# A hybrid state-space, mLSTM and expert-lookup block on one core: log-sigmoid chain turned to tokens on partitions, table products dealt out in pairs, last norm per tile

## The chip, the cores and the metric

The kernel runs on one core of one Trainium2 chip. The metric is the device time of one execution in microseconds (us), median of three runs. The engines are called as in the profile: PE (TensorE), DVE (VectorE), ACT (ScalarE), POOL (GpSimd) and SP (SyncE, which here only issues transfers).

## What is computed

One decoder layer on 512 tokens, with 16 learned meta tokens ahead of them (T = 528), width 1024, all in float32:

```python
xn = rmsnorm(h, norm1_g)
u_s, x_m, z_m, g_s, g_m = split(xn @ w_in)
y_s = s5_branch(u_s) @ w_ssm_out                       # diagonal complex state space, gelu, GLU
xc  = silu(causal_conv(x_m))                           # 4 taps per channel
q, k, v = blockdiag(xc, wq), blockdiag(xc, wk), blockdiag(x_m, wv)
gates = concat(q, k, v) @ w_if + b_if
log_i, log_f = gates[..., :H], log_sigmoid(gates[..., H:])     # H = 4 heads
h_m = mlstm(q, k, v, log_i, log_f);  h_m = headnorm(sigmoid(z_m) * h_m) + skip * xc
h = h + (sigmoid(g_s) * y_s + sigmoid(g_m) * (h_m @ w_ml_out)) @ w_out
h = h + peer_ffn(rmsnorm(h, norm2_g))                  # 16 of 128*128 experts for each of 8 heads
out = rmsnorm(h, final_norm_g)[:, 16:]
```

The S5 branch makes its transition and input matrices from parameters, in the kernel: tables w1 (inputs to chunk states) and l3 (chunk states to outputs) are outer products of a [128 x 16 x 16] coefficient and powers of the discretized eigenvalue.

## The kernel before, in words

Two functions follow one another. `front` (about 0 to 500 us) holds everything up to the second norm, `peer` the rest. Every float32 product is done as three matmuls on numbers split into a high and a low part (`mm3`, `proj`: high by high, high by low, low by high; lines 82 to 86 and 343 to 346). `wblock` (L156) loads one 128x1024 block of weights into one of two buffers, splits it with ACT (L78, high part) and DVE or POOL (L79, low part); a running number of the block decides between DVE and POOL. Numbers 21 to 28 are the blocks of the GLU (`wglu`), of the S5 output (`wso`) and the first two of z (`wz0`); all of these go to POOL.

Inside `front` the parts that the change touches are, in order of the program:

- `xmproj(b)` (mLSTM input, block b of 8; two PSUM tiles xm, evacuated by DVE with the norm's factor, L430) and `gsgate(b)` (gate of the S5 branch; PSUM tile gs, evacuated by DVE into `mix`, then a sigmoid on ACT, L480). The projections share four PSUM buffers.
- `outer` (L410): six multiplications or sums of [128 x 2048] for w1, later six for l3 (r and i parts, with one scratch tile t), and at L503 a sign change of l3's imaginary part, all on DVE. `l1part` transposes w1 on PE.
- the chunk states: v on PE, `turn` (L507, twice, around two scans) on DVE; then y (tables l1, l2t, l3 by inputs and states) on PE.
- `conv(b)` (L433): three DVE steps (L436), a sigmoid on ACT into one shared scratch tile (profile name qt, L439), one DVE multiplication by it.
- y is copied from PSUM by ACT (`ys`, L567), written to memory (`yd`, L571), read back in another layout (`yt`, L573), and goes through gelu and the GLU (`yg`, `ygh`, `y2h`, `y2l`).
- the gates' weights `wgt` (split in place of a part of the states' tile) and the gate sums on PE (`gate`, L594), from the split conv outputs `xp`.
- after the GLU, the log-sigmoid of four gate rows: a chain of some 20 DVE steps on [4 x 528] tiles (`rwa`, `rwb`, L625 to L639; Abs and Exp on ACT at L626 and L627), two scans (L645, L646), then the S5 output `so` on PE with its DVE evacuations into `mix`, the first z products, and per 128 tokens a short chain `dv`, `crs` on DVE (L688, L689, and a tensor_tensor) whose four results PE transposes into `cbp` (L694 to L697). The mLSTM's v follows on PE (`vm` L740, `v` L748).

In `peer`, three token tiles of 128 go through all 16,384 experts as dense products on PE, key row by key row (`h`, `o`; 128 rows j, each with a 512 KB load of `v` on SP's queue, L1400, a split into vh by ACT and vl by DVE); for the other 128 tokens, POOL gathers rows of u and v (L1015, six buffers), and DVE accumulates them into `ac` (L1029). Loads of the last stage are tied to a row of this loop by `after(ins, j)`, an order without a wait. At the end the o products of the last rows are made tile by tile, and the last norm runs on DVE and ACT for token tiles (0), (1) and (2, 3) together: residual add (L1445), squares with sum (L1446, ACT), product with the gain (L1447), ten one-column steps for the reciprocal root (L91 to L105), scaling of one half on DVE (L1456) and one on ACT (L1454), two output transfers (L1457).

A scheduler orders each engine's instructions from the program's order and from dependences; `later(ins, on)` adds such an order without a wait.

Of the kernel before, what the change touches and what calls it, by code (L numbers as in the profile page):

```python
# [23 lines left out]
P = 128  # L24
# [102 lines left out]
def front(tc, a, dbg, cst, dram, xnp, ident, h2d, gds, x0, qt01, dump, split, mm3, rsqrt, rsqrt_cols):  # L127
# [3 lines left out]
    with es:  # L131
# [24 lines left out]
        def wblock(src, name, nk=NK):  # L156

            raw = wp.tile([P, NK, P], F32, tag="wraw", name=f"{name}_w", bufs=2)
            SY.dma_start(raw[:, :nk] if len(src.shape) == 3 else raw.rearrange("p (b k) n -> p b k n", b=2), src)
            hi = wp.tile([P, NK, P], F32R, tag="whi", name=f"{name}_h")  # L160
            lo = wp.tile([P, NK, P], F32R, tag="wlo", name=f"{name}_l")
            nblk[0] += 1
            i_ = split(hi[:, :nk], lo[:, :nk], raw[:, :nk], GP if nblk[0] == 2 or nblk[0] > 12 and (nblk[0] % 2 or nblk[0] > NG) else V)
# [257 lines left out]
        def xmproj(b):  # L421
            if b % 4 == 0:
                xmt.append(half(f"xmt{b // 4}", f"xmt{b // 4}"))
                xct.append(half(f"xct{b // 4}", f"xct{b // 4}"))
            hi, lo = wblock(a["w_in"][4 + b], f"wx{b}")
            xm, xc = xmt[b // 4][:, b % 4], xct[b // 4][:, b % 4]
            for h in range(2):
                p = pmm(f"xm{b}{h}", (P, T // 2))
                proj(hi, lo, p, lambda k: [x[k // 4][:, k % 4, h * 264:(h + 1) * 264] for x in (xnh, xnl)])
                tt(xm[:, h * 264:(h + 1) * 264], p, nt[:, h * 264:(h + 1) * 264], OP.mult)  # L430
            A.activation(xc, xm, AF.Identity, scale=convw[:, b, 3:4], bias=convb[:, b:b + 1])

        def conv(b):  # L433
            xm, xc = xmt[b // 4][:, b % 4], xct[b // 4][:, b % 4]
            for s_ in (1, 2, 3):
                V.scalar_tensor_tensor(xc[:, s_:], xm[:, :T - s_], convw[:, b, 3 - s_:4 - s_], xc[:, s_:],  # L436
                                       op0=OP.mult, op1=OP.add)
# [35 lines left out]
        def gsgate(b):  # L473
            hi, lo = wblock(a["w_in"][20 + b], f"wgs{b}")
            p = pmm(f"gs{b}")
            for k in range(NK):
                mm3(p, hi[:, k], lo[:, k], xnh[k // 4][:, k % 4, NM:], xnl[k // 4][:, k % 4, NM:], k == 0, k == NK - 1)
            o = mix[b // 4][:, b % 4]
            tt(o, p, nt[:, NM:], OP.mult)
            A.activation(o, o, AF.Sigmoid)  # L480
        for b in range(2):
            xmproj(b)
            l1part(b)
            gsgate(b)

# [6 lines left out]
        for x in range(2):  # L492
            for q0, q1 in ((0, 7), (7, 14), (14, 16)):
# [5 lines left out]
                A.copy(vs[:, x, q0:q1], p[:, :q1 - q0])  # L499
        xmproj(2)  # L500
        gsgate(2)
        outer(*l3, c_r, c_i, pw_r[:, :, 1:], pw_i[:, :, 1:], (OP.subtract, OP.add))
        V.tensor_scalar(l3[1], l3[1], -1.0, None, op0=OP.mult)  # L503

        rt = half("rt", "pBi", (P, 2, NP_, NC_))

        def turn(o, v, sg):  # L507

            for x in range(2):
                tt(o[:, x], v[:, x], phs[0], OP.mult)  # L510
                tt(sct, v[:, 1 - x], phs[1], OP.mult)
                tt(o[:, x], o[:, x], sct, OP.add if (x == 0) == (sg < 0) else OP.subtract)
        turn(rt, vs, -1)
# [3 lines left out]

        st = rt
        turn(st, vs, 1)
        for q in range(4):  # L520
            gkpart(q)
        xmproj(3)
        gsgate(3)
# [97 lines left out]
        dump("ys_glu", yg)  # L621
        rwb = half("rwb", "pE")[:H]
        y2_, z_, lf = (rwb[:, n] for n in range(3))

        later(V.tensor_scalar(xf, xf, bif[:, 1:2], None, op0=OP.add), lo_)  # L625
        A.activation(e_, xf, AF.Abs)  # L626
        A.activation(e_, e_, AF.Exp, scale=-1.0)  # L627
        V.tensor_scalar(y_, e_, 2.0, None, op0=OP.add)
        for h in range(2):
            c = slice(h * 264, (h + 1) * 264)  # L630
            V.reciprocal(y_[:, c], y_[:, c])
        tt(y_, y_, e_, OP.mult)
        tt(y2_, y_, y_, OP.mult)
        V.tensor_scalar(z_, y2_, 1.0 / 15, None, op0=OP.mult)
        for n in (13, 11, 9, 7, 5, 3):
            V.scalar_tensor_tensor(z_, z_, 1.0 / n, y2_, op0=OP.add, op1=OP.mult)
        V.scalar_tensor_tensor(z_, z_, 1.0, y_, op0=OP.add, op1=OP.mult)
        V.tensor_scalar(xf, xf, 0.0, None, op0=OP.min)
        V.scalar_tensor_tensor(lf, z_, -2.0, xf, op0=OP.mult, op1=OP.add)  # L639
        rst, fl, mr = e_, y_, y2_  # L640
        V.memset(rst, 1.0)
        ST = [0] + [NM + i * P for i in range(NT)] + [T]
        for s0 in ST[:-1]:
            V.memset(rst[:, s0:s0 + 1], 0.0)
        V.tensor_tensor_scan(fl, rst, lf, 0.0, op0=OP.mult, op1=OP.add)  # L645
        V.tensor_tensor_scan(mr, lf, li, 0.0, op0=OP.add, op1=OP.max)  # L646
        dump("li", li)
        dump("lf", lf)
        dump("mr", mr)
        tt(li, li, fl, OP.subtract)  # L650
        em = z_
        tt(amu, fl, mr, OP.subtract)
        A.activation(em, mr, AF.Exp, scale=-1.0)
        dv = small("dv", (H, NT + 1))
        V.memset(dv, 0.0)
        for b in range(NK):
# [288 lines left out]
def peer(tc, a, out, dbg, cst, dram, xh, xl, blanks, ident, h2d, gds, x0, qt01, dump, split, mm3, rsqrt_cols):  # L945
# [21 lines left out]
    with es:  # L967
# [419 lines left out]
        for j in range(NKEY):  # L1387
# [51 lines left out]

        for of in ((0,), (1,), (2, 3)):  # L1440
            ss = fin.tile([P, 2, 2], F32, name=f"ss3{of[0]}")
            for n, i in enumerate(of):
                y, x = hr[i], op_[i - 1] if i else ac0
                for c in range(2):
                    order(V.tensor_tensor(y[:, cc[c]], x[:, cc[c]], y[:, cc[c]], op=OP.add))  # L1445
                    A.activation(jq, y[:, cc[c]], AF.Square, scale=1.0 / math.sqrt(D), accum_out=ss[:, c, n:n + 1])  # L1446
                order(V.tensor_tensor(sq[i], y, gf, op=OP.mult))  # L1447
            m = len(of)
            rstd = rsqrt_cols(fin, ss[:, 0, :m], m, f"n3{of[0]}", more=ss[:, 1, :m])
            for c in range(2):  # L1450
                for n, i in enumerate(of):
                    o, x, r_ = hr[i][:, cc[c]], sq[i][:, cc[c]], rstd[:, n:n + 1]
                    if c:
                        A.activation(o, x, AF.Copy, scale=r_)  # L1454
                    else:
                        V.tensor_scalar(o, x, r_, None, op0=OP.mult)  # L1456
                    (SY, A)[c].dma_start(out[i * P:(i + 1) * P, cc[c]], o)  # L1457

# [64 lines left out]
```

## Time and profile before

| | us |
|---|---|
| median of three runs | 1733.84 |
| lowest, highest | 1731.15, 1735.12 |
| the profiled execution, its own time | 1735.74 |
| its span from first to last instruction | 1734.0 |
| PE busy, DVE busy, POOL busy, ACT busy | 1661.3, 1329.4, 722.7, 707.9 |

The time of an execution is that of the device, the span lies 1.7 us below it. The busy times are sums over the whole span; the kernel has stages with different limits, so they are a first look only.

### The profile page before, as it was taken

The page shows a single profiled execution, that of the slowest core. Times are in us where ns is not written, and L with a number is a line of the kernel's source. Part 1 is how long each engine was busy: PE and PEld are TensorE (multiplying, and loading weights), DVE is VectorE, ACT ScalarE, POOL GpSimd, SP SyncE. Part 2 cuts the span into 40 slices and gives each one's busy share as a digit, 9 for nine tenths or more (in the row PEclk, how much of TensorE's full clock was granted, in tenths as well). Part 3 has the DMA queues.
Part 4 walks back from the last instruction along what each step waited for, and adds up shares of the span by engine and source line. Part 5 has one row for each costly group of instructions (what it writes and reads, how often), then busy time and mean ns, then how long its engine had stood idle before and what let it go on. Part 6 is the DMA issues. An engine that isn't in the chain of part 4 may idle for free.

```text
span 1734.0 us, 25541 instructions
## 1 busy us (share of the span) xinstructions
PE 1661.3 (96%) x9376; PEld 1471.6 (85%) x9376; DVE 1329.4 (77%) x2601; ACT 707.9 (41%) x1037; POOL 722.7 (42%) x494
## 2 busy tenths in 40 slices
PE   7899889999999999999999999999999999999992
PEld 6798677877888899999999988888888888888871
DVE  6996783356468899977884688788888888888888
ACT  4454516543332334456664343333333333333321
POOL 2022532214123278888885134333333333343452
PEclk9999989999999999999999999999999999999996
DMA  4513243212442336689999999999999999999894
GB/s 179 117 50 98 75 157 118 77 49 73 167 182 99 124 73 183 163 265 295 300 303 341 348 348 343 346 339 349 335 346 349 336 344 333 349 336 333 296 343 170
DMA packets 172774, 408.79 MB, mean 236 GB/s; under 512 B 44392, under 2 KB 89576, under 8 KB 171496
## 3 DMA queue, kind: packets, MB, share of 16 engines
q1 hardware_dynamic: 108816, 264.40, 43.2%
q0 software_dynamic: 55328, 134.31, 23.2%
q10 hardware_dynamic: 8504, 8.44, 1.6%
q8 instruction: 73, 1.20, 0.3%
q14 instruction: 53, 0.43, 0.1%
HBM read 359.81 MB, written 47.28 MB: 235 GB/s over the span
## 4 chain that ended last, share of the span: by engine, by line
PE 80%; DVE 11%; DMA 4%; ACT 2%; issue 2%; POOL 1%; SPq 0%; POOLq 0%; ACTq 0%; DVEq 0%
PE h L82 10%; PE h L85 10%; PE h L86 10%; PE o L85 10%; PE o L86 10%; PE o L82 10%; PE gp L1304 2%; PE q L85 2%; PE q L86 2%; PE q L82 2%; DMA wo<-in_w_out 1%; PE s L820 1%; PE n L829 1%; DMA v<-in_v 1%; PE gm L343 1%
## 5 line engine op out<-in xcount | busy, mean ns | idle before, releaser
L82 PE MATMUL h<-x2h,uh 128*128 128x384 f32 x1024 | 345.6, 337 | 0.0
L86 PE MATMUL h<-x2h,ul 128*128 128x384 f32 x1024 | 343.3, 335 | 0.0
L85 PE MATMUL h<-x2l,uh 128*128 128x384 f32 x1024 | 343.2, 335 | 0.0
L85 PE MATMUL o<-vl,wh 128*128 128x512 f32 x768 | 301.0, 392 | 0.8 <-DVE vl L79 0.8
L86 PE MATMUL o<-vh,wl 128*128 128x512 f32 x768 | 300.0, 392 | 0.0
L82 PE MATMUL o<-vh,wh 128*128 128x512 f32 x768 | 295.8, 391 | 3.4 <-ACT vh L78 3.4
L1238 POOL DMA_INDIRECT gds<-gw,ix x128 | 238.9, 1867 | 47.1 <-issue 36.6
L1015 POOL DMA_INDIRECT g<-in_v,e x128 | 161.2, 1260 | 229.3 <-PE o L86 78.4
L78 ACT ACTIVATE uh<-u 128x1024 fp32r<-128x1024 f32 x128 | 136.0, 1062 | 250.6 <-PE h L85 198.1
L1015 POOL DMA_INDIRECT g<-in_u,e x103 | 130.4, 1266 | 254.5 <-DVE jk L1022 122.1
L79 DVE TENSOR_TENSOR ul<-u,uh 128x1024 fp32r<-128x1024 f32 x128 | 156.4, 1222 | 73.0 <-ACT uh L78 58.8
L78 ACT ACTIVATE wh<-w 128x384 fp32r<-128x384 f32 x128 | 67.1, 525 | 329.5 <-issue 265.8
L85 PEld LDWEIGHTS h<-x2l,uh 128*128 128x128 f32 x1024 | 192.3, 188 | 2.2
L82 PEld LDWEIGHTS h<-x2h,uh 128*128 128x128 f32 x1024 | 192.3, 188 | 2.3
L86 PEld LDWEIGHTS h<-x2h,ul 128*128 128x128 f32 x1024 | 192.2, 188 | 0.7
L82 PEld LDWEIGHTS o<-vh,wh 128*128 128x128 f32 x768 | 144.8, 189 | 33.0 <-ACT vh L78 3.9
L79 DVE TENSOR_TENSOR vl<-v,vh 128x1024 fp32r<-128x1024 f32 x128 | 156.2, 1221 | 18.8 <-ACT vh L78 17.0
L85 PEld LDWEIGHTS o<-vl,wh 128*128 128x128 f32 x768 | 144.8, 189 | 30.1 <-DVE vl L79 1.1
L86 PEld LDWEIGHTS o<-vh,wl 128*128 128x128 f32 x768 | 144.9, 189 | 29.9
L1029 DVE SCALAR_TENSOR_TENSOR ac<-g,w,ac 128x1024 f32<-128x1024 f32 x127 | 162.6, 1280 | 2.3 <-DMA g<-in_v,e 1.2
L78 ACT ACTIVATE vh<-v 128x1024 fp32r<-128x1024 f32 x128 | 133.5, 1046 | 15.2 <-PE o L86 9.8
L79 DVE TENSOR_TENSOR wl<-w,wh 128x384 fp32r<-128x384 f32 x128 | 71.5, 558 | 84.6 <-ACT wh L78 81.6
(526 smaller groups left out, 3089.8 us busy)
## 6 DMA issues: line engine op xcount, KB each, us to landing
u<-in_ut SPq DMA_DIRECT2D x128, 512.0 KB
v<-in_v SPq DMA_DIRECT2D x128, 512.0 KB
gd<-stg SPq DMA_DIRECT2D x8, 2048.0 KB
gi<-gd SPq DMA_DIRECT2D x16, 1024.0 KB
ad<-act SPq DMA_DIRECT2D x80, 192.0 KB
acl<-ad SPq DMA_DIRECT2D x80, 192.0 KB
gds<-qt SPq DMA_DIRECT2D x8, 1024.0 KB
gi<-gds SPq DMA_DIRECT2D x16, 512.0 KB
```

What stands on the lines that cost most here:

```text
L78: A.activation(hi, src, AF.Copy)
L79: return eng.tensor_tensor(lo, src, f32(hi), op=OP.subtract)
L82: i_ = PE.matmul(ps, lh, rh, start=first, stop=False)
L85: PE.matmul(ps, lh, rl, start=False, stop=False)
L86: return PE.matmul(ps, ll, rh, start=False, stop=last)
L343: i_ = PE.matmul(ps_, hi[:, k], rh, start=k == 0, stop=False)
L820: PE.matmul(p[:, :w], xk[kk][:, c0:c0 + P], qt[:, kk, T - w:], start=kk == 0, stop=kk == 1)
L829: PE.matmul(p, pm[:, OFF[j] + (i - j) * P:OFF[j] + (i - j + 1) * P], vt[:, j], start=j == 0, stop=False)
L1015: return GP.indirect_dma_start(out=t, out_offset=None, in_=a["u"] if s_ < P else a["v"], in_offset=bass.IndirectOffsetOnAxis(ap=e0[:, c:c ...
L1029: i_ = V.scalar_tensor_tensor(ac0, g, w0[:, c:c + 1], ac0, op0=OP.mult, op1=OP.add)
L1238: i_ = GP.indirect_dma_start(out=gds.rearrange("b i j t -> (b i j t)").unsqueeze(1), out_offset=bass.IndirectOffsetOnAxis(ap=ix[:, c:c + 1 ...
L1304: PE.matmul(p[:, t], o1[:, a_, :, b_], ow[:, n, a_, :, b_], start=n == 0, stop=n == 1)
```

## The change

1. Weight blocks 21 to 28 are split by DVE in place of POOL.
2. The twelve `outer` steps are dealt out in pairs, each pair held behind an evacuation of a projection (two behind xmproj(0), gsgate(0), xmproj(1), xmproj(2), gsgate(2), xmproj(3)). The imaginary part of l3 is made with its sign, so the step of L503 goes. Both `l1part` stand behind xmproj(1).
3. The 24 conv steps are held behind the last step of the second turn (`turned`).
4. The log-sigmoid chain stands right behind the gate sums. PE transposes the [4 x 528] row into five groups of [128 x 4] tokens (the last one overlaps the fourth), the chain runs on [128 x 20], five transposes bring it back. Two scans, `li`, `amu` and Exp follow in program order there.
5. The last o products run by halves of 512 columns, the last norm tile by tile with the gain's product by halves, and four reciprocal roots in place of three. The loads of the residual rows `hr` (4 x 512 KB on SP's queue) are tied to rows 122, 122, 123, 123 of the loop in place of 120.

```diff
-            i_ = split(..., GP if nblk[0] == 2 or nblk[0] > 12 and (nblk[0] % 2 or nblk[0] > NG) else V)
+            i_ = split(..., GP if nblk[0] == 2 or nblk[0] > NG + 8 or 12 < nblk[0] <= NG and nblk[0] % 2 else V)
...
-        def outer(o_r, o_i, x_r, x_i, y_r, y_i, sums):
-            for o, a_, b_, c_, d_, op in ((o_r, x_r, y_r, x_i, y_i, sums[0]), (o_i, x_r, y_i, x_i, y_r, sums[1])):
-                tt(o, every(a_), every(b_), OP.mult)
-                tt(t3, every(c_), every(d_), OP.mult)
-                tt(o, o, t3, op)
-        outer(*w1, bb_r, bb_i, pv_r, pv_i, (OP.subtract, OP.add))
+        outers = [(w1[0], ...), (w1[1], ...), (l3[0], c_r, pw1_r, c_i, pw1_i, OP.subtract),
+                  (l3[1], nc_i, pw1_r, c_r, pw1_i, OP.subtract)]
+        def outer(on):
+            for _ in range(2):
+                later(tt(*outers.pop(0)), on)
...
         for b in range(2):
-            xmproj(b)
-            l1part(b)
-            gsgate(b)
+            outer(xmproj(b))
+            if b:
+                l1part(0)
+                l1part(1)
+            outer(gsgate(b)) if not b else gsgate(b)
...
-        V.tensor_scalar(l3[1], l3[1], -1.0, None, op0=OP.mult)
...
-            conv(b)
+            conv(b, turned)
...
+        xtp = ptr("xtp", (P, 5, H))
+        XC = [0, P, 2 * P, 3 * P, T - P]
+        for n, c0 in enumerate(XC):
+            PE.transpose(xtp[:, n], xf[:, c0:c0 + P], ident[:H, :H])
+        V.tensor_copy(xt_, xtp)
+        A.activation(et_, xtp, AF.Abs)
+        A.activation(et_, et_, AF.Exp, scale=-1.0)
...
+        for n in range(5):
+            PE.transpose(lfp[n // 4][:, n % 4 * P:(n % 4 + 1) * P], xt_[:, n], ident)
+        A.copy(lf[:, :S], lfp[0])
+        V.tensor_copy(lf[:, S:], lfp[1][:, P - NM:P])
...
-                    for n in range(NKEY - LAST, NKEY):
-                        products(i, *ops[n], tc.keep_in_program_order if i else None)
+                    for c in range(2):
+                        for n in range(NKEY - LAST, NKEY):
+                            products(i, *ops[n], tc.keep_in_program_order if i or c else None, (c,))
...
-            after(SY.dma_start(hr[i], h2d[i * P:(i + 1) * P]), NKEY - 8)
+            after(SY.dma_start(hr[i], h2d[i * P:(i + 1) * P]), NKEY - 6 + i // 2)
...
-        for of in ((0,), (1,), (2, 3)):
+        for i in range(NT):
```

ACT around the copies of y (`ys`), where the conv's sigmoids (`qt<-xct`) stand, before:

```order
L439 ACTIVATE qt_68<-xct_1212 128x528 x2
L567 COPY ys<-y_1471 128x8x64
L567 COPY ys<-y_1472 128x8x64
L567 COPY ys<-y_1523 128x8x64
L567 COPY ys<-y_1524 128x8x64
L571 DMA yd<-ys 16x32x64 x4
```

and now:

```order
L573 COPY ys<-y_1470 128x8x64
L573 COPY ys<-y_1471 128x8x64
L443 ACTIVATE qt_68<-xct_566 128x528
L78 ACTIVATE xp_1620<-xct_566 128x528
L443 ACTIVATE qt_68<-xct_1211 128x528
L78 ACTIVATE xp_1620<-xct_566 128x528
L443 ACTIVATE qt_68<-xct_1211 128x528 x3
L573 COPY ys<-y_1522 128x8x64
L573 COPY ys<-y_1523 128x8x64
L577 DMA yd<-ys 16x32x64 x4
```

The sigmoids that before are spread among earlier work now stand between and ahead of the ys copies; the last two ys copies, and behind them the transfers to `yd`, follow the eighth sigmoid.

DVE behind the last GLU product, where the log-sigmoid chain (`rwa`, `rwb`) begins, before:

```order
L625 TENSOR_SCALAR rwa<-rwa,bif 4x528
L638 TENSOR_SCALAR rwa<-rwa 4x528
L628 TENSOR_SCALAR rwa<-rwa 4x528
L631 RECIPROCAL rwa<-rwa 4x264 x2
L181 TENSOR_TENSOR mix_570<-so_1989,mix_570 128x8x64
L181 TENSOR_TENSOR mix_570<-so_2003,mix_570 128x8x64
L181 TENSOR_TENSOR mix_570<-so_2023,mix_570 128x8x64
L181 TENSOR_TENSOR rwa<-rwa 4x528
L181 TENSOR_TENSOR mix_570<-so_2037,mix_570 128x8x64
L181 TENSOR_TENSOR rwb<-rwa 4x528
L641 MEMSET rwa 4x528
L634 TENSOR_SCALAR rwb<-rwb 4x528
```

and now:

```order
L617 COPY rwb<-xtp 128x20
L628 TENSOR_SCALAR rwb<-rwb 128x20
L79 TENSOR_TENSOR wso_l<-wso_w,wso_h 128x1024
L181 TENSOR_TENSOR yg<-yg,sglu_1991 128x512
L620 TENSOR_SCALAR rwb<-rwb 128x20
L621 RECIPROCAL rwb<-rwb 128x20
L181 TENSOR_TENSOR rwb<-rwb 128x20
L79 TENSOR_TENSOR y2l<-yg,y2h 128x512
L181 TENSOR_TENSOR rwb<-rwb 128x20
L624 TENSOR_SCALAR rwb<-rwb 128x20
L626 SCALAR_TENSOR_TENSOR rwb<-rwb 128x20 x6
L627 SCALAR_TENSOR_TENSOR rwb<-rwb 128x20
```

The [4 x 528] steps with their two reciprocals, which stood ahead of the evacuations of `so`, are [128 x 20] steps now, and stand among the last steps of the GLU.

SP's queue at the end (`qt<-in_gf` is the load of the last norm's gain, L1400 and L1416 are the loads of v), before:

```order
L1400 DMA v_16110<-in_v 128x1024
L1427 DMA qt_68<-in_gf 128x1024
L1431 DMA hr_16191<-h2d 128x1024
L1431 DMA hr_16192<-h2d 128x1024
L1431 DMA hr_16193<-h2d 128x1024
L1431 DMA hr_16194<-h2d 128x1024
L1400 DMA v_16122<-in_v 128x1024
```

and now:

```order
L1416 DMA v_16123<-in_v 128x1024
L1444 DMA qt_68<-in_gf 128x1024
L1416 DMA v_16135<-in_v 128x1024
L1448 DMA hr_16204<-h2d 128x1024
L1448 DMA hr_16205<-h2d 128x1024
L1448 DMA hr_16206<-h2d 128x1024
L1448 DMA hr_16207<-h2d 128x1024
```

The load of v for the last key row has passed the four loads of the residual rows.

## Rows read from the trace of the kernel before

**Rows 1.** The page's busy times: engine, busy us, share, instructions.

```profile
PE 1661.3 (96%) x9376; PEld 1471.6 (85%) x9376; DVE 1329.4 (77%) x2601; ACT 707.9 (41%) x1037; POOL 722.7 (42%) x494
```

**Rows 2.** Busy time by stretch: stretch, its us, PE, PEld, DVE, ACT, POOL, PEclk, DMA share, GB/s.

```profile
72.50:77.60 5.10, 0.40 (x2) 0.02 (x1) 5.10 (x4) 1.01 (x2) 0.00 (x0) 0.99 0.00 0
77.60:84.30 6.70, 6.42 (x15) 4.94 (x16) 6.70 (x8) 1.60 (x3) 0.00 (x0) 0.50 0.47 157
...
214.20:217.40 3.20, 3.18 (x7) 1.99 (x8) 3.20 (x4) 0.00 (x0) 1.17 (x1) 0.50 0.64 237
...
241.30:251.60 10.30, 6.77 (x57) 5.96 (x61) 6.77 (x20) 2.85 (x5) 3.67 (x4) 0.50 0.84 282
```

**Rows 3.** PE's waits, 60 to 90 us, then 200 to 252 us: total us, times, longest.

```profile
PE xm L343 <- DVE mix L181: 4.7, 1, 4.7
...
PE cbp L694 <- DVE crs L181: 5.3, 3, 3.3
PE so L343 <- DVE mix L181: 2.7, 1, 2.7
PE so L343 <- ACT y2h L78: 0.9, 1, 0.9
```

**Rows 4.** DVE's timeline, tables and conv: start, us, instruction, idle before and releaser.

```profile
74.58 2.29 DVE L181 TENSOR_TENSOR w1i<-s5p 128x2048 f32<-128x2048 f32 x1
...
98.37 4.13 DVE L181 TENSOR_TENSOR t<-parb,pw_r 128x2048 f32<-128x2048 f32 x1
...
109.49 1.21 DVE L503 TENSOR_SCALAR l3i<-l3i 128x2048 f32<-128x2048 f32 x1
...
153.70 0.71 DVE L181 TENSOR_TENSOR xct<-xct,qt 128x528 f32<-128x528 f32 x1 [0.77 <-ACT qt L439]
```

**Rows 5.** ACT's timeline from the last conv sigmoid to the gate's weights.

```profile
153.02 0.64 ACT L439 ACTIVATE qt<-xct 128x528 f32<-128x528 f32 x1 [2.13 <-DVE xct L436]
...
155.37 1.07 ACT L567 COPY ys<-y 128x512 f32<-128x512 f32 x2 [0.75 <-PE y L564]
156.48 4.34 ACTq L571 DMA_DIRECT2D yd<-ys  x4
...
164.17 0.23 ACT L78 ACTIVATE wgt<-wgs 128x32 fp32r<-128x32 f32 x1 [7.72 <-DMA yd<-ys]
```

**Rows 6.** PE's timeline, the first gate sums.

```profile
165.50 2.16 PE L594 MATMUL gate<-xp,wgt 128*100 128x264 f32 x16 [0.21 <-DVE wgt L79]
```

**Rows 7.** DVE's timeline at the end of the GLU and the chain's reciprocals.

```profile
202.06 2.42 DVE L181 TENSOR_TENSOR yg<-yg,sglu 128x512 f32<-128x512 f32 x1 [0.83 <-ACT sglu L618]
...
209.50 3.45 DVE L631 RECIPROCAL rwa<-rwa 4x264 f32<-4x264 f32 x2
```

**Rows 8.** The chain that ended last: start, us, piece; v on PE, then the last load of v.

```profile
247.50 3.71 PE v L748 x16
251.97 1.98 PE v L748 x16
...
1669.54 17.47 DMA v<-in_v
```

**Rows 9.** SP's timeline at the end.

```profile
1666.14 2.16 SPq L1431 DMA_DIRECT2D hr<-h2d  x4
1669.54 0.33 SPq L1400 DMA_DIRECT2D v<-in_v  x1
```

**Rows 10.** DVE's timeline at the end: last split of v, accumulations, norm.

```profile
1688.20 1.23 DVE L79 TENSOR_TENSOR vl<-v,vh 128x1024 fp32r<-128x1024 f32 x1 [3.98 <-ACT vh L78]
...
1701.18 10.67 DVE L1029 SCALAR_TENSOR_TENSOR ac<-g,w,ac 128x1024 f32<-128x1024 f32 x8 [1.23 <-DMA g<-in_v,e]
...
1716.68 1.28 DVE L1445 TENSOR_TENSOR hr<-o,hr 128x512 f32<-128x512 f32 x2
...
1721.46 1.28 DVE L1445 TENSOR_TENSOR hr<-o,hr 128x512 f32<-128x512 f32 x2
...
1728.35 0.88 DVE L1456 TENSOR_SCALAR hr<-sq,n32o 128x512 f32<-128x512 f32 x2
```

More of the change, by code (lines that the diff above doesn't have):

```diff
@@ L162, in wblock @@
             nblk[0] += 1
-            i_ = split(hi[:, :nk], lo[:, :nk], raw[:, :nk], GP if nblk[0] == 2 or nblk[0] > 12 and (nblk[0] % 2 or nblk[0] > NG) else V)
+            i_ = split(hi[:, :nk], lo[:, :nk], raw[:, :nk], GP if nblk[0] == 2 or nblk[0] > NG + 8 or 12 < nblk[0] <= NG and nblk[0] % 2 else V)
             if nblk[0] > NG + 6 and blank:
@@ L429, in xmproj, with conv @@
                 proj(hi, lo, p, lambda k: [x[k // 4][:, k % 4, h * 264:(h + 1) * 264] for x in (xnh, xnl)])
-                tt(xm[:, h * 264:(h + 1) * 264], p, nt[:, h * 264:(h + 1) * 264], OP.mult)
+                i_ = tt(xm[:, h * 264:(h + 1) * 264], p, nt[:, h * 264:(h + 1) * 264], OP.mult)
             A.activation(xc, xm, AF.Identity, scale=convw[:, b, 3:4], bias=convb[:, b:b + 1])
-        def conv(b):
+            return i_
+        def conv(b, on):
             xm, xc = xmt[b // 4][:, b % 4], xct[b // 4][:, b % 4]
             for s_ in (1, 2, 3):
-                V.scalar_tensor_tensor(xc[:, s_:], xm[:, :T - s_], convw[:, b, 3 - s_:4 - s_], xc[:, s_:],
-                                       op0=OP.mult, op1=OP.add)
+                later(V.scalar_tensor_tensor(xc[:, s_:], xm[:, :T - s_], convw[:, b, 3 - s_:4 - s_], xc[:, s_:],
+                                             op0=OP.mult, op1=OP.add), on)
             sg = zero[:, :T]
@@ L499, in front @@
                 A.copy(vs[:, x, q0:q1], p[:, :q1 - q0])
[L500 to L503 removed]
+        outer(xmproj(2))
+        outer(gsgate(2))
         rt = half("rt", "pBi", (P, 2, NP_, NC_))
@@ L511, in turn @@
                 tt(sct, v[:, 1 - x], phs[1], OP.mult)
-                tt(o[:, x], o[:, x], sct, OP.add if (x == 0) == (sg < 0) else OP.subtract)
+                i_ = tt(o[:, x], o[:, x], sct, OP.add if (x == 0) == (sg < 0) else OP.subtract)
+            return i_
         turn(rt, vs, -1)
@@ L518, in front @@
         st = rt
-        turn(st, vs, 1)
+        turned = turn(st, vs, 1)
         for q in range(4):
             gkpart(q)
-        xmproj(3)
+        outer(xmproj(3))
         gsgate(3)
@@ L542, in front @@
         for b in range(4):
-            conv(b)
+            conv(b, turned)
         for b in range(4, NK):
             xmproj(b)
-            conv(b)
+            conv(b, turned)
         GP.memset(zero, 0.0)
@@ L597, in front @@
             A.activation(li[:, c], gp[h][64:64 + H], AF.Identity, bias=bif[:, 0:1])
-            V.tensor_copy(xf[:, c], gp[h][96:96 + H])
+            V.tensor_scalar(xf[:, c], gp[h][96:96 + H], bif[:, 1:2], None, op0=OP.add)
             tt(li[:, c], li[:, c], gp[h][0:H], OP.add)
             tt(xf[:, c], xf[:, c], gp[h][32:32 + H], OP.add)
+        rwb = half("rwb", "pE")
+        y2_, z_, lf = (rwb[:H, n] for n in range(3))
+        xt_, et_, yt_, y2t, zt_ = (
+            rwb[:, 3, 5 * H * n:5 * H * (n + 1)].rearrange("p (n h) -> p n h", h=H) for n in range(5))
+        xtp = ptr("xtp", (P, 5, H))
[5 more added lines that the diff above has]
+        A.activation(et_, et_, AF.Exp, scale=-1.0)
+        V.tensor_scalar(yt_, et_, 2.0, None, op0=OP.add)
+        V.reciprocal(yt_, yt_)
+        tt(yt_, yt_, et_, OP.mult)
+        tt(y2t, yt_, yt_, OP.mult)
+        V.tensor_scalar(zt_, y2t, 1.0 / 15, None, op0=OP.mult)
+        for n in (13, 11, 9, 7, 5, 3):
+            V.scalar_tensor_tensor(zt_, zt_, 1.0 / n, y2t, op0=OP.add, op1=OP.mult)
+        V.scalar_tensor_tensor(zt_, zt_, 1.0, yt_, op0=OP.add, op1=OP.mult)
+        V.tensor_scalar(xt_, xt_, 0.0, None, op0=OP.min)
+        V.scalar_tensor_tensor(xt_, zt_, -2.0, xt_, op0=OP.mult, op1=OP.add)
+        lfp = [ptr(f"lfp{n}", (H, S)) for n in range(2)]
+        for n in range(5):
+            PE.transpose(lfp[n // 4][:, n % 4 * P:(n % 4 + 1) * P], xt_[:, n], ident)
+        A.copy(lf[:, :S], lfp[0])
+        V.tensor_copy(lf[:, S:], lfp[1][:, P - NM:P])
+        rst, fl, mr = e_, y_, y2_
+        V.memset(rst, 1.0)
+        ST = [0] + [NM + i * P for i in range(NT)] + [T]
+        for s0 in ST[:-1]:
+            V.memset(rst[:, s0:s0 + 1], 0.0)
+        V.tensor_tensor_scan(fl, rst, lf, 0.0, op0=OP.mult, op1=OP.add)
+        V.tensor_tensor_scan(mr, lf, li, 0.0, op0=OP.add, op1=OP.max)
+        dump("li", li)
+        dump("lf", lf)
+        dump("mr", mr)
+        tt(li, li, fl, OP.subtract)
+        em = z_
+        tt(amu, fl, mr, OP.subtract)
+        A.activation(em, mr, AF.Exp, scale=-1.0)
+        dv = small("dv", (H, NT + 1))
+        V.memset(dv, 0.0)
         mix.append(half("mix1", "mix1", (P, 4, S)))
@@ L621, in front @@
         dump("ys_glu", yg)
[L622 to L655, printed above, removed]
         for b in range(NK):
@@ L1377, in peer, with products @@
         ops = []
-        def products(i, j, wh, wl, vh, vl, pin=None):
+        def products(i, j, wh, wl, vh, vl, pin=None, halves=(0, 1)):
             s_ = slice(i * P, (i + 1) * P)
-            for c in range(2):
+            for c in halves:
                 cc = slice(c * 512, (c + 1) * 512)
@@ L1438, in order @@
             return i_
-        for of in ((0,), (1,), (2, 3)):
[L1441 to L1449, printed above, removed]
-            for c in range(2):
[L1451 to L1457, printed above, removed]
+        for i in range(NT):
+            ss = fin.tile([P, 2], F32, name=f"ss3{i}")
+            y, x = hr[i], op_[i - 1] if i else ac0
+            for c in range(2):
+                order(V.tensor_tensor(y[:, cc[c]], x[:, cc[c]], y[:, cc[c]], op=OP.add))
+                A.activation(jq, y[:, cc[c]], AF.Square, scale=1.0 / math.sqrt(D), accum_out=ss[:, c:c + 1])
+                order(V.tensor_tensor(sq[i][:, cc[c]], y[:, cc[c]], gf[:, cc[c]], op=OP.mult))
+            rstd = rsqrt_cols(fin, ss[:, 0:1], 1, f"n3{i}", more=ss[:, 1:2])
+            for c in range(2):
+                o, x = y[:, cc[c]], sq[i][:, cc[c]]
+                if c:
+                    A.activation(o, x, AF.Copy, scale=rstd)
+                else:
+                    V.tensor_scalar(o, x, rstd, None, op0=OP.mult)
+                (SY, A)[c].dma_start(out[i * P:(i + 1) * P, cc[c]], o)
 def prepare(inputs):
```

8 lines of the change are left out of this document (7 added, 1 removed).

## The prediction, made before the change was run

> **What bounds the kernel now.** I read the page first, then busy time by stretch, then PE's waits, then the timelines of the engines that PE waits for, and the chain of waits for the end. The page [rows 1] has PE busy for 1661.3 us of 1734.0, so only some 70 us can be had anywhere, and they must be looked for where PE stands still or runs slowly. The waits before 260 us are few [rows 3]: 4.7 us for the evacuation of a gate tile into `mix`, 5.3 for `crs`, 2.7 for `mix` again, 0.9 for `y2h`. [...] Later, to the last key row, the change touches nothing; what is gained or lost before it shifts that stage as a whole. At the end, PE is done early and DVE sets the time [rows 10].
>
> **The table products and the conv.** Before, `mix` is evacuated at 76.8 us behind table products of about 2.2 us each [rows 4]; the wait that follows costs PE 4.7 us, and the half clock 6.7 x 0.5 = 3.35 more. In the new order four table products stand ahead of it in place of five, and no conv step; with 2.2 us less for the one and about 0.7 for each conv step, most of the wait goes, and PE reaches y up to 8 us earlier. That gain I cost at **nothing**, because something else is late next. Before, the last ys copies waited 0.75 us for y on PE [rows 5], but the last conv sigmoid was only just ahead of them (153.02). Now that sigmoid is a condition: the last two ys copies stand behind the eighth sigmoid on ACT, and behind them wait the transfers to `yd`, the reading back, the gate's weights and PE's gate sums (165.50, [rows 6]). The round trip from the first of these transfers to the weights is 164.17 - 156.48 = 7.7 us [rows 5], unchanged. So the gate follows the end of the conv, which is the end of DVE's work in this stretch: 153.70 + 0.71 = 154.4 [rows 4].
>
> What moves that end: the sign step goes (-1.2 [rows 4]), and the last idle 0.77 goes. The eight sigmoids share one scratch tile with their multiplications; four of the pairs now stand with nothing between, so 0.64 + 0.71 in series where before only the 0.71 counted: 4 x 0.64 = +2.6. Two DVE steps now stand right behind ACT work that comes late (the low part of a weight block, the turn's first steps behind the copies of the states); each I take at an ACT copy, 1.07 [rows 5], +2.1. The clears of the scans' tile move ahead of the conv; I take half of one 0.71 step [rows 4], +0.4. The conv then ends 3.1 us later. The last sigmoid stands one 0.71 before that end and the two copies (1.07) follow it: 154.4 + 3.1 - 0.7 + 1.1 = 157.9, against 156.4 before. **Term: +1.5.** Bounds: -2.3, if the two late waits do not appear (-2.1) and the POOL collision that makes one table product 4.13 in place of 2.29 goes (-1.8, [rows 4]); +6, if the other four pairs are in series too (+2.6) and the turn loses as much again in waits that the conv steps filled.
>
> **PE's new gap.** Before, PE had 10 us of gate products between y's end and the gate (165.5 - 155.4). Those start 8 us earlier now, while the gate starts later: a gap of about 10 us in front of the gate. [...] **Term: +3.4**, bounds 0 (another engine ends last in the stretch behind it, so that a slow PE costs nothing) and +5.2. [...]
>
> **The log-sigmoid chain.** Before, it runs in front of and among the `so` evacuations, with two reciprocals of 3.45 us [rows 7], and is done too late for `crs`. On [128 x 20] a step has 20 columns in place of 528 and lies in DVE's idle time of the GLU. Of the waits [rows 3] 5.3 + 2.7 = 8.0 go; the 0.9 for `y2h` I leave, since Abs, a table load and Exp now stand ahead of the last `y2h` on ACT. The half clock behind the `mix` wait goes (3.2 x 0.5 = 1.6). The first v products come back to the time of the second, 3.71 - 1.98 = 1.7 [rows 8]. The `yg` product that collides with a POOL split takes 2.42 [rows 7] and would take about the 0.71 of a free step: 1.7. **Term: -13.0.** The eight splits that move from POOL lie beside the GLU, where DVE waits for ACT and PE; if the four that stand among `so` and z each cost a free split, taken as half a 2.29 step [rows 4], 4 x 1.15 = 4.6 are lost (bound -8.4). If the 0.9 goes as well, it is -13.9.
>
> **The end.** The four loads of residual rows stand ahead of v's last load on SP's queue (1666.14 against 1669.54, [rows 9]); that load takes 17.47 us to land [rows 8], and DVE idles 3.98 before it splits it [rows 10]. With v first, the split and all 16 accumulations behind it can start up to 3.98 earlier. A wait of 1.23 for a gather stays, as the six gather buffers still come free one by one. **Term: -4.0**, bounds 0 (the gathers' transfers take the room) and -5.2. The residual rows land late but have until about 1708.
>
> The norm takes 1721.46 - 1716.68 = 4.8 us for one tile alone, and 1728.35 + 0.88 - 1721.46 = 7.8 for the last two together [rows 10]; those become 9.6, +1.8. Halving the gain's product lets DVE reach the root before ACT has summed the second square: an ACT pass over 528 columns takes 0.64 [rows 5], half a pair of DVE steps as much [rows 10], so the wait is a part of 0.64; I take 0.25 for each of four tiles, +1.0. The last scaling on DVE is one half in place of two, -0.4. **Term: +2.4**, bounds +1.2 (no wait) and +3.4 (0.5 for each).
>
> **Sum:** +1.5 + 3.4 - 13.0 - 4.0 + 2.4 = -9.7. From the profiled execution's 1735.74 that is 1726.0; the median of the three runs is 1.9 lower, so the forecast is **1724.1**.
>
> **The rivals.**
> *The new gap gives it all back.* If conv and turn end 10 us later than I think, or PE's slow stretch reaches far into the GLU, the gate's delay eats the chain's gain: 1733.8 - 9.7 + 9.7, about 1731 to 1736. For it: DVE has no idle time before 154 us but the 0.77, so anything that it waits for there is paid. Against: the table pairs now fill that stretch.
> *Slower: the turn without cover.* The 24 conv steps filled DVE's waits in the turn's chain of copies, scans and products; now all stand behind its last step. Each us that DVE then idles ahead of that step arrives at the gate one for one. The point from which this decides is 9.7 us for no gain and 13.2 for a loss beyond what a measurement tells; with 17 us of idle time, all 24 steps at 0.71 uncovered, the time is 1724.1 + 17 = 1741. Against: the order keeps evacuations, table copies and splits in between.
> *The gate is not held.* If the sigmoids keep up and ys goes out as soon as y is there, the 8 us gained at y arrive, and +1.5 + 3.4 fall away: 1724.1 - 12.9 = 1711. Against it stands ACT's order.
> *The residual rows' move does nothing.* Then 4.0 are missing: 1728.1.
>
> **Chances.** A measurement of this kernel tells 0.2%, 3.5 us, from no change. The forecast has 0.62, the idle move at the end 0.14 and the free gate 0.06, all faster by more than that: 0.82. Giving it back has 0.11, the uncovered turn 0.07. The terms' ends all together would be 1713 and 1740; they don't fall together. The range 1715 to 1731.5 takes in the idle move at the end and about half of each unknown; out of it fall most of the free gate, the uncovered turn and half of the give-back, some 0.18.
>
> **What would show it.** Right: no wait of xm for `mix` near 75 us; PE idle for some 10 us ahead of the first gate sum, and PEclk 0.50 behind it; that sum at 166 to 169 us; no waits for `crs`; both first v groups at 2.0 us; the last split of v about 4 us earlier against the end of PE's main loop; four tiles of some 5 us each in the norm. Wrong: a gate before 162 or after 173, `crs` waits that stay, or a last load of v that still lands 17 us after its issue.

## The result, and the profile after

The changed kernel takes 1723.59 us (median of 4 runs, 1721.68 to 1724.69) against 1733.82 for the kernel before: ratio 0.9942, 95% interval 0.9925 to 0.9959, so 10 us faster by the medians. The profiled execution takes 1724.69 us, with a span of 1722.7; it is 11.05 faster than the profiled execution before (1735.74).

The page of the changed kernel, its busy times [rows 1]:

```profile
PE 1656.1 (96%) x9386; PEld 1469.4 (85%) x9386; DVE 1318.6 (77%) x2622; ACT 707.4 (41%) x1038; POOL 708.1 (41%) x486
```

PE's waits from 90 us on, of the changed kernel (total us, times, longest), which answer to [rows 3]:

```profile
PE gate L600 <- DVE wgt L79: 7.4, 1, 7.4
PE xm L346 <- POOL wx_l L79: 2.3, 1, 2.3
...
PE so L343 <- DVE mix L181: 0.4, 1, 0.4
```

The waits for `crs` and `y2h` are gone, that for `mix` at `so` is down from 2.7 to 0.4, and that for `mix` near 75 us is gone too (the longest wait of PE from 60 to 90 us is now 0.2). Two are new: 2.3 us for a POOL split of a weight block, and 7.4 us ahead of the first gate sum. Busy time by stretch (its columns are those of [rows 2]) shows the granted clock behind the first of the two new waits, and in and behind the second:

```profile
122.40:125.60 3.20, 3.20 (x15) 3.20 (x15) 3.20 (x9) 0.83 (x1) 0.00 (x0) 0.50 0.51 164
159.60:167.20 7.60, 0.16 (x2) 0.04 (x1) 0.54 (x4) 0.70 (x4) 0.87 (x2) 0.75 0.90 175
167.20:170.50 3.30, 3.30 (x16) 3.30 (x17) 1.24 (x3) 2.67 (x4) 1.52 (x1) 0.55 1.11 215
170.50:180.00 9.50, 9.50 (x51) 7.96 (x50) 5.71 (x7) 8.11 (x10) 3.95 (x3) 1.00 0.21 62
```

ACT's timeline from the conv's sigmoids to the gate's weights [rows 5], and PE's first gate sum [rows 6]:

```profile
153.47 0.64 ACT L443 ACTIVATE qt<-xct 128x528 f32<-128x528 f32 x1 [0.24 <-DVE xct L181]
155.23 0.65 ACT L443 ACTIVATE qt<-xct 128x528 f32<-128x528 f32 x1 [1.12 <-DVE xct L181]
156.65 0.65 ACT L443 ACTIVATE qt<-xct 128x528 f32<-128x528 f32 x1 [0.78 <-DVE xct L181]
157.20 1.06 ACT L573 COPY ys<-y 128x512 f32<-128x512 f32 x2
158.29 4.37 ACTq L577 DMA_DIRECT2D yd<-ys  x4
...
165.97 0.23 ACT L78 ACTIVATE wgt<-wgs 128x32 fp32r<-128x32 f32 x1 [7.71 <-DMA yd<-ys]
```

```profile
149.88 0.39 PE L570 MATMUL y<-rt,l3i 64*128 64x64 f32 x4
...
167.19 3.51 PE L600 MATMUL gate<-xp,wgt 128*100 128x264 f32 x16 [7.44 <-DVE wgt L79]
```

y is done on PE at 150.3 (155.3 before), yet its last copies start at 157.2, right behind the eighth sigmoid, and each of the last sigmoids waits for a multiplication by the one before it. DVE's timeline, the log-sigmoid chain in its new form and place [rows 7], and the last `crs`:

```profile
204.99 0.28 DVE L621 RECIPROCAL rwb<-rwb 128x20 f32<-128x20 f32 x1
...
206.42 1.25 DVE L626 SCALAR_TENSOR_TENSOR rwb<-rwb 128x20 f32<-128x20 f32 x6
...
231.07 0.67 DVE L181 TENSOR_TENSOR crs<-rwa,dv 4x512 f32<-4x512 f32 x1
```

`crs` is done at 231.7, ahead of PE's first use at 237.3. The chain of work that ended last, at the two v groups [rows 8]:

```profile
239.74 2.15 PE v L764 x16
...
242.46 1.98 PE v L764 x16
```

The end, on SP's queue [rows 9] and on DVE [rows 10]:

```profile
1660.49 0.33 SPq L1416 DMA_DIRECT2D v<-in_v  x1
1664.88 4.97 SPq L1448 DMA_DIRECT2D hr<-h2d  x4
```

```profile
1674.38 1.23 DVE L79 TENSOR_TENSOR vl<-v,vh 128x1024 fp32r<-128x1024 f32 x1 [0.39 <-ACT vh L78]
1675.52 10.60 DVE L1045 SCALAR_TENSOR_TENSOR ac<-g,w,ac 128x1024 f32<-128x1024 f32 x8
1687.03 7.89 DVE L1045 SCALAR_TENSOR_TENSOR ac<-g,w,ac 128x1024 f32<-128x1024 f32 x6 [0.91 <-DMA g<-in_v,e]
...
1697.95 0.69 DVE L1461 TENSOR_TENSOR hr<-ac,hr 128x512 f32<-128x512 f32 x1
...
1703.16 0.68 DVE L1461 TENSOR_TENSOR hr<-o,hr 128x512 f32<-128x512 f32 x1
...
1718.33 0.48 DVE L1470 TENSOR_SCALAR hr<-sq,n33o 128x512 f32<-128x512 f32 x1
```

DVE waits 0.39 in place of 3.98 for the last split of v. A tile of the norm takes 1703.16 - 1697.95 = 5.2 us in place of 4.8.

To tell front and end apart I use one fixed point: the split of v's row 100, from which PE's loop runs at the same pace in every execution (rows 120 and 124 follow it 116.6 and 137.1 us later in all profiles).

| us | before | after | difference |
|---|---|---|---|
| start to split of v's row 100 | 1535.22 | 1526.18 | -9.04 |
| from there (row 100) to the last split of v | 152.98 | 148.20 | -4.78 |
| from the last split to the first residual add | 23.68 | 23.57 | -0.11 |
| from the first residual add to the end of the span | 22.12 | 24.75 | +2.63 |

The front varies between executions of one code by some 5 us in this measure (1521.3 to 1526.2 in four profiles with the changed front), so single terms of it are read from medians or from stretches in which both profiles do the same.

### The profile page after: what moved, and what is told of

It reads as the page before. It is cut to its first block, busy times and chain, and to the rows that moved or that the text cites. A ratio compares the mean times of both kernels' runs of the same rounds, so it can differ in the third digit from the quotient of the medians.

```text
span 1722.7 us, 25574 instructions
## 1 busy us (share of the span) xinstructions
PE 1656.1 (96%) x9386; PEld 1469.4 (85%) x9386; DVE 1318.6 (77%) x2622; ACT 707.4 (41%) x1038; POOL 708.1 (41%) x486
## 4 chain that ended last, share of the span: by engine, by line
PE 85%; DVE 7%; DMA 3%; ACT 2%; issue 1%; POOL 1%; ACTq 0%; POOLq 0%; DVEq 0%
PE h L82 10%; PE h L85 10%; PE h L86 10%; PE o L85 10%; PE o L86 10%; PE o L82 10%; PE gp L1320 2%; PE q L86 2%; PE q L85 2%; PE q L82 2%; DMA wo<-in_w_out 1%; DVE xct L440 1%; PE s L836 1%; PE n L845 1%; PE gm L343 1%
```

## The experiments

All were timed in five rounds beside the kernel before, whose medians were 1733.8 to 1734.2.

**The last norm as before** (`t_norm`):

```diff
-        for i in range(NT):
+        for of in ((0,), (1,), (2, 3)):
...
-                order(V.tensor_tensor(sq[i][:, cc[c]], y[:, cc[c]], gf[:, cc[c]], op=OP.mult))
+                order(V.tensor_tensor(sq[i], y, gf, op=OP.mult))
```

> The changed kernel, with only the last norm put back to the form before: tiles (0), (1) and (2, 3) together. My theory: the norm per tile is the one part of the change that costs. The span from the first residual add to the end was 22.1 us before (1711.88 to 1734.0) and is 24.75 now (1697.95 to 1722.7); four tiles of 5.2 us in place of 4.8, 4.8 and 7.8. Put back, the time falls by 2.6 us, to about 1721.0, and nothing ahead of the norm moves. Rival: smaller last pieces let the output transfers end sooner, so that four chains cost no more than three; then the time stays within 0.7 us of 1723.6.

Measured: 1720.93 (ratio 0.9920, 0.9907 to 0.9933), 2.7 below the changed kernel; from the first add to the end 22.15 us again. That is what was expected: the norm per tile costs what its rows say.

**The residual rows' loads as before** (`t_hr`):

```diff
-            after(SY.dma_start(hr[i], h2d[i * P:(i + 1) * P]), NKEY - 6 + i // 2)
+            after(SY.dma_start(hr[i], h2d[i * P:(i + 1) * P]), NKEY - 8)
```

> The changed kernel, with only the four loads of the residual rows put back to row 120, ahead of the last load of v. My theory: v's last load lands some 4 to 5 us later, DVE idles before its last split as before (about 4 us), all 16 accumulations start that much later: +4.8 us, about 1728.4. Rival: the accumulations are bound by the gathers (POOL's issues and their transfers), of which the residual rows only change the order; then the waits for gathers shrink by what the split loses, and the time rises by under 1.5 us.

Measured: 1724.14 (0.9952, 0.9938 to 0.9967; 1722.31 to 1730.35), only 0.5 above. ACT's timeline of this run, the last split of v:

```profile
1672.10 1.06 ACT L78 ACTIVATE vh<-v 128x1024 fp32r<-128x1024 f32 x1 [3.57 <-DMA v<-in_v]
```

The wait for v's load is back as expected, and the last split comes 151.88 us after row 100's in place of 148.20. The load lands 16.4 us after its issue here; in `t_norm`, which leaves it ahead of the residual rows, ACT's split begins 12.8 us after the issue and has waited for no load. The first residual add comes 2.6 later, not 3.7, as the waits for gathers shrank from 1.3 to 0.2 us. The median shows less than that: my number was missed, and the rival's (under 1.5) was met. Its interval and that of the changed kernel overlap by more than the difference, so this run alone leaves the size open (`log_hr` below gives it).

**The log-sigmoid chain as before** (`t_log`), its lines moved back behind the GLU and to [4 x 528], the rest as changed:

> The changed kernel, with the log-sigmoid chain put back: on [4 x 528], behind the GLU. [...] Rival: part of what the chain gained is owed to the splits moved from POOL to DVE, which no longer collide with crs and yg; then it rises by 6 to 9 us only.

Measured: 1731.32 (0.9985, 0.9976 to 0.9993), 7.7 above the changed kernel: less than I expected (11 to 13 more, 1735 to 1737), and inside the rival's range (6 to 9). PE's waits of this run:

```profile
PE cbp L700 <- DVE crs L181: 5.1, 4, 4.0
...
PE so L343 <- DVE mix L181: 1.9, 3, 1.2
```

They come back, the longest at `mix` is 1.2 in place of 2.7. The chain is three quarters of the whole gain, even beside all other parts.

Why not more? By the rival, the splits that moved from POOL to DVE own a share, and the timeline fits it. DVE in this run:

```profile
201.61 0.68 DVE L181 TENSOR_TENSOR yg<-yg,sglu 128x512 f32<-128x512 f32 x1
...
207.33 3.45 DVE L637 RECIPROCAL rwa<-rwa 4x264 f32<-4x264 f32 x2
```

The last `yg` product takes 0.68 us in place of 2.42 [rows 7], and the reciprocals start 21.1 us behind the first GLU product (186.24) in place of 24.1 (209.50, behind 185.44). Busy time from the first GLU product to the first q product behind the v groups (columns of [rows 2]): before, then `t_log`, `log_only` (described below) and the changed kernel.

```profile
185.44:258.45 73.01, 64.02 (x403) 53.43 (x402) 59.04 (x90) 21.77 (x30) 30.05 (x19) 0.91 0.39 130
186.24:255.58 69.34, 61.96 (x403) 52.07 (x402) 58.38 (x97) 22.06 (x29) 12.74 (x11) 0.95 0.41 137
185.33:247.76 62.43, 62.03 (x413) 52.41 (x412) 44.37 (x84) 21.28 (x31) 29.55 (x19) 0.97 0.45 153
187.77:248.95 61.18, 60.43 (x414) 50.98 (x413) 44.35 (x91) 21.37 (x30) 11.11 (x11) 1.00 0.46 155
```

With the old chain the stretch is 3.7 us shorter when the splits are on DVE; with the new chain 1.2 (3.1 in `w_pool`), where executions of one front differ by 1.6 (61.1 to 62.7). So the two edits seem to take away in part the same waits. No run moves the splits alone.

**The last sigmoids behind the copies of y** (`ys_held`; in the program the conv steps of blocks 4 to 7 move with them; the lines are shortened, their comments are mine):

```diff
-            conv(b, turned)                      # b = 4 to 7, behind xmproj(b)
...
+        for b in range(4, NK):                   # behind the transfers of yd
+            sgd = conv(b, turned, i_)            # its sigmoid: later(..., i_)
...
+            if t_ % 2:
+                later(i_, sgd)                   # yt's transfers on ACT's queue
```

> The changed kernel, with one order turned round: the last four conv sigmoids on ACT stand behind the copies of y and the issues of their transfers, not ahead of them. My theory: the gate's start at 167.2 us is set by the eighth sigmoid on ACT, to which y (done on PE at 150.3) waits, and not by the data that the gate sums read; the first gate sum comes at 157 to 160, PE's gap of 7.4 us in front of it goes with its half clock, and the GLU starts 5 to 9 us sooner: 1715 to 1719. Rival: the gate sums and the GLU need the conv's last blocks anyway, so the wait only moves to the later gate sums (or to the gelu's input, whose reading back now waits for the last sigmoid): less than 2 us gained.

Measured: 1720.64 (0.9920, 0.9907 to 0.9933), 2.9 faster than the changed kernel: more than the rival's 2, less than my 1715 to 1719. Counted from the first y product on PE (134.0 here, 135.4 in the changed kernel's profile), the first gate sum comes 7.7 us earlier (158.1), the GLU 4.7 (181.6), and the first z product 0.4 (223.9). PE's waits of this run:

```profile
PE gate L606 <- DVE xp L79: 2.4, 4, 1.7
PE xm L346 <- POOL wx_l L79: 2.3, 1, 2.3
PE gate L606 <- DVE wgt L79: 2.1, 1, 2.1
```

So ACT's order did hold the gate, as the theory says. But the gain at the end is not what the gate moved. It lies nearer to what PE's waits shrank, from 7.4 to 2.1 + 2.4: the gate sums only moved ahead of products of `gs` that come later now.

**Conv not held behind the turn** (`c_free`; `later` left out of `conv`):

> The changed kernel, with the conv steps no longer held behind the second turn. My theory: DVE's work up to the conv's end is the same sum, so the gate moves little: the four sigmoid and multiplication pairs in series (some 2.6 us) go, the turn and with it y come later, and PE's gap before the gate shrinks. The gate starts 0 to 2.5 us sooner, the time is 1721 to 1724. Rival: the hold is what brings y forward; without it y is late again and DVE and PE both wait, and the time rises by 3 us or more.

Measured: 1723.65 (0.9947, 0.9934 to 0.9960), no change, within what was expected. But the gate does not start sooner: y ends on PE at 159.0 in place of 150.3, and the first gate sum comes at 169.1. The GLU starts at 179.1, 8.7 us sooner than in the changed kernel's profile, the first z product only 1.2. The gap before the gate is gone, and others take its place (2.0 us for `mix`, 1.8 for `xtp`, 1.3 for `y2l`, 1.0 for `rt`).

**Table products as before** (`o_old`; the old `outer`, called twice, and the sign step):

> The changed kernel, with the table products put back (w1's six at once, l3's six and the sign step behind the gate of block 2, none held). [...] Rival: dealing the products out is part of the gain, as PE's lost 8 us reach the gate: 1728 or more.

Measured: 1725.01 (0.9953, 0.9940 to 0.9965), 1.4 above, within what I expected (1723.6 to 1725.5, with up to 4.7 us of waiting near 75 us). That wait is only 1.2 here (the conv steps, which stood ahead of it before, are not back), so this run tests the wait only in part; `log_only`, which has all of it, is the better test.

**Weight splits given back to POOL** (`w_pool`; the old condition in `wblock`):

> The changed kernel, with the splits of the weight blocks 21 to 28 given back to POOL. My theory: of the gain of the log chain's stretch only the collisions depend on them (a yg product of 2.4 us against 0.7, crs steps of 2.4 to 2.8 against 0.2): the time rises by 1 to 3 us. Rival: on DVE the splits take the room of the so evacuations (so's four late evacuations were 1.25 each), so that giving them back frees DVE and gains 1 us or more.

Measured: 1723.44 (0.9936, 0.9923 to 0.9949), no difference: neither the 1 to 3 us that I expected nor the rival's gain. The collisions do come back (a `yg` product of 2.23 us, a scan of 3.38 in place of 1.22), but only waits of 0.7 and 0.6 reach PE.

**Last sigmoids and norm together** (`ys_norm`):

> Both edits together: the last conv sigmoids behind the copies of y, and the last norm in the form before. They touch stages 1500 us apart, so by my theory their gains add: 2.6 us below the first edit alone, 1712.5 to 1716.5 if that one brings what I expect. Rival: the gather stage takes back what the front gives, because the gathers and loads near the end are paced by transfers; then less than the sum.

Measured: 1719.73 (0.9927, 0.9915 to 0.9939). Both stages show their gain in the profile (z at 222.4, 22.17 us from the first add to the end); the median is 0.9 below the first edit alone, outside the expected range, less than 2.6 and within the spread of the two (1719.96 to 1721.73, 1718.36 to 1724.06).

**The log-sigmoid chain alone, on the kernel before** (`log_only`): lines 604 to 650 of the changed kernel put into it in place of the old ones, nothing else.

> The kernel before, with the log-sigmoid chain alone moved behind the gate sums and turned to tokens on partitions; splits, table products, conv and the end as before. My theory by now: PE is the bound of this stretch too, and the time follows the sum of PE's idle and half-clock time; the chain alone removes the waits for mix and crs and the slow spells behind them, 9 to 12 us, and the wait near 75 us stays but is no longer made up by a gap before the gate. So 1722 to 1726, as fast as the whole change but for the end. Rival: table products, conv hold and splits carry a share; then only 5 to 8 us, 1726 to 1729.

Measured: 1722.60 (0.9933, 0.9920 to 0.9946), 11.2 faster than before, as expected. One edit gives as much as the whole change. PE's waits of this run, 50 to 262 us:

```profile
PE xm L343 <- DVE mix L181: 4.7, 1, 4.7
PE xm L346 <- DVE wx_l L79: 1.0, 1, 1.0
PE gate L594 <- POOL xp L79: 0.9, 2, 0.5
...
PE gate L594 <- DVE wgt L79: 0.3, 1, 0.3
```

The 4.7 us for `mix` are there as before, and PE goes through to the gate (0.3 us). In the change, the table products' new places take the 4.7 away, and 7.4 in front of the gate take their place. The edit changes two things at once, the chain's place and its shape, and no run separates them. Summed over the DVE timelines, the chain's steps ahead of the scans are 12.1 us in the old shape (`t_log`) and 3.0 in the new (the changed kernel), so the old shape in the new place would need some 9 us more of DVE, as an estimate; what that costs is open.

**The chain and the residual rows' loads, on the kernel before** (`log_hr`; `log_only` and the one line of `t_hr` turned round):

> The same with the four loads of the residual rows moved behind the last load of v, and nothing else: the two edits that by my theory carry the gain, without the norm per tile, which costs. If they add, it is 2 to 4 us faster than the chain alone, 1719 to 1723, and faster than the whole change by the norm's 2.6. Rival: the residual rows' move is worth under 1 us, as the medians of the undoing had it.

Measured: 1719.35 (0.9905, 0.9891 to 0.9919), 3.3 below the chain alone and 4.2 below the whole change, as expected: the lowest median of all, with two of the change's parts (`ys_norm` is 0.4 behind it, which is no difference).

**The front alone** (`front_only`: loads, last products and norm as before):

> The changed kernel, with the whole end put back (loads, products by tile, norm for (0), (1), (2, 3)). By the two traces the front gives 9.0 us (start of the split of v's row 100: 1535.2 before, 1526.2 now) and the end 2.3 on balance. So 1724 to 1726. Rival: the end is worth nothing (+2.6 of the norm takes all that the loads give): 1723 to 1724.

Measured: 1724.05 (0.9942, 0.9929 to 0.9955), 9.7 faster than before. It lies on the border of both expectations and does not tell them apart.

**The end alone, on the kernel before** (`tail_only`):

> The kernel before, with the changed end alone. By the traces -4.9 for the accumulations' start and +2.6 for the norm: 1731 to 1732.5. Rival: the loads' move gains under 2 us at the end, since the gathers' waits take the rest; then 1733.5 to 1735, no gain or a loss.

Measured: 1732.50 (0.9991, 0.9982 to 1.0000), 1.3 faster, as expected: what the loads give, less the norm (-1.3 - 2.7 = -4.0 for the loads). The profile has 148.20 us from row 100 to the last split, and 24.73 from the first add to the end.

Over all profiles, the last split comes 151.2 to 153.0 us after row 100's where the residual rows are loaded ahead of v (4 profiles), and 148.20 where they are loaded behind it (10 profiles). The first add comes 174.3 to 176.7 against 171.0 to 172.6 us after row 100's split.

## Why the prediction was right

The forecast was 1724.1, the result 1723.6. The mechanisms were right in the main; that the sum is out by only 0.5 is in part luck, since the new gap was priced too high and so was the chain's gain, and the two errors have opposite signs. In the one profile the terms measure +1.7 (table products and conv), +0.6 (gap), -11.8 (chain and splits), -4.9 (loads) and +2.6 (norm); with +0.5 more between the first q product and row 100 that makes -11.3 of span, against -9.7 forecast and 10.2 by the medians.

- **Table products and conv, +1.5.** Right in its mechanism: the last three multiplications wait 0.7 us each for a sigmoid on the same scratch tile, and the gate follows the conv's end. That end came at 158.0 (forecast 157.5), but at 155.7 to 155.8 in three other profiles with the same front (`t_norm`, `t_hr`, `front_only`), so the half microsecond is luck. The two late waits, 2.1 in the sum, were not where the prediction put them: the turn's first step waited 0.18, and 1.70 was lost ahead of the first table product, for ACT's `s5p`. The first gate sum came at 167.2, +1.7, in this profile, and at 164.9 to 165.1 in the three others, 0.5 earlier than before; the term is +1.7 at most.
- **The gain at y at nothing.** Right as far as the medians tell: `front_only` with the dealt products is no faster than `log_only` without them (1724.05 and 1722.60). The reason was put too narrowly, though. A shift of the gate is not passed on in full: with the gate 7.7 us earlier (`ys_held`) the end came 2.9 earlier. What fits the runs better is PE's time without work or at half clock: 4.7 + 3.35 us went near 75 us, and 7.4 + 2.3, in this profile each with a short stretch at half clock, came.
- **PE's new gap, +3.4.** Over-priced. The 3.4 is half of the 6.7 us at a clock of 0.50 behind the wait near 75 us, and the bound of 5.2 half of the 10.3 around the `crs` waits [rows 2]; no run shows that a gap ahead of the gate costs either. What the profile shows is a stretch at half clock behind the gap of 3.3 us in place of 6.7 (2.8 to 6.2 in the three others), and from the first gate sum to the GLU it took 20.58 us against 19.94, +0.6 (20.3 to 21.6 in the three others, +0.3 to +1.7). The rows show where the rest went: over the 7.6 us around the wait the granted clock is 0.75, over the first 3.3 us of work 0.55, and 1.00 behind them, so a part of the slow stretch passed while PE had no work; before, the clock was still at 0.99 in the wait [rows 2]. With the term above, the two were to give +4.9 at the GLU's start; it came at 185.1 to 187.8 in the four profiles, against 185.4 before.
- **The log-sigmoid chain, -13.0.** Right in its mechanism, too large by 1 to 3: -11.2 as the median of `log_only`, and -10.3 to -11.9 from the first GLU product to the first q product in the four profiles. Two pieces are over-sized. "The first v products come back to the time of the second": they took 2.2 us in this profile, but 3.6 in that of `log_only`, without any wait ahead of them (below). And the collision of `yg` with POOL, 1.7 in the sum, is DVE's time, added to waits of PE that the sum had already taken out; with the new chain, giving the splits back to POOL costs nothing (`w_pool`). Taken out of the changed kernel, the chain is worth 7.7 (`t_log`), since the moved splits then do a part of its work.
- **The loads' move, -4.0.** Right: -3.3 by the medians of `log_hr` and `log_only`, -4.0 by `tail_only` less the norm, -4.8 at the last split in the profile of the change. The cause is shown by the wait for v's load, which comes and goes with that one line. `t_hr` shows less in its median (0.5); why is not settled. Its runs spread over 8 us.
- **The norm, +2.4.** +2.6 in the profile, +2.7 by `t_norm`. The size is right, its parts less so: the four tiles take 3.5 us more of DVE's time (forecast +2.8), and the outputs end 3.9 us behind DVE's last step in place of 4.8, -0.9 (forecast -0.4).

Of the rivals, "the new gap gives it all back" was the nearest: the gap came, and took back about what the table products had won (`front_only` is 1.4 above `log_only`, with intervals that overlap). "The turn without cover" did not happen: DVE idles 0.18 us ahead of the turn's first step, not at all within it, and 0.72 behind its last. "The residual rows' move does nothing" fell by `log_hr`. "The gate is not held" was refuted by the order, as the prediction said, and `ys_held` shows that with the gate 7.7 us earlier it gives 3 us, and not the 13 that the prediction put on it.

## What to carry to other kernels

Where one engine is the bound of a stretch, sum its waits and its slow-clock time there; a wait removed early in the stretch is a gain only if no wait of the same engine grows in its place. Do not add to this sum the time of another engine that the waits already hold, and expect two edits that remove the same wait to be worth less together than the sum of each alone. Before trusting a change of several parts, run its strongest part alone: here one part gave as much as all five, and two of them made a faster kernel than the whole. A chain of small steps on four of 128 partitions, moved ahead of where it is needed and turned, was worth 11 us for ten transposes and three copies; which of the two, the move or the turn, brings how much is not shown.

## What the runs showed of the hardware that was not expected

**The clock fell without a wait.** Busy time by stretch of `log_only`, around the small `cbp` transposes and the first v group:

```profile
230.00:236.40 6.40, 6.40 (x62) 6.14 (x60) 0.00 (x0) 1.75 (x3) 4.46 (x5) 1.00 0.83 268
236.40:240.50 4.10, 4.10 (x35) 3.70 (x33) 2.18 (x14) 2.31 (x5) 2.46 (x2) 0.62 0.74 260
240.50:246.00 5.50, 5.50 (x75) 4.81 (x78) 4.40 (x11) 0.00 (x0) 1.27 (x3) 0.97 0.59 214
```

PE has work throughout, yet the granted clock falls to 0.62 behind 1.8 us of transposes of four rows. In the changed kernel's profile the same place keeps 1.00, in that of `t_norm`, whose front is the same code, it falls to 0.69. Of the eleven profiles with the new chain five show the fall (a first v group of 3.3 to 3.6 us) and six do not (2.2 us), so it costs 1.1 to 1.4 us, in some executions. That the tiny products bring it about is a guess from their place; what decides between two executions is not shown.

**A POOL split beside DVE products.** POOL's timeline of the changed kernel, two splits of the same size:

```profile
111.44 10.87 POOL L79 TENSOR_TENSOR wx_l<-wx_w,wx_h 128x1024 fp32r<-128x1024 f32 x1 [12.33 <-ACT wx_h L78]
130.86 2.76 POOL L79 TENSOR_TENSOR wgs_l<-wgs_w,wgs_h 128x1024 fp32r<-128x1024 f32 x1 [8.55 <-ACT wgs_h L78]
```

Beside the turn's products and a scan, which DVE runs without a pause (it is busy for 10.81 of the 10.87 us), the split takes 10.87 us in place of 2.76, and PE waits 2.3 us for it. DVE's own steps keep their length in this time (the scan 2.34 us, as the one just before it; four products 1.24) but for the last product, which takes 2.23; where the time goes within the split is not shown.
